# Instance norm over 512 volumes: rows of 48 KiB in four slots in place of 32 KiB in six, and the odd eight instances moved to the start

## The chip, the cores and the metric

One core of one Trainium2 chip runs the whole program; the other cores are idle. The time is the device time of one execution in microseconds. A time below is the median of some runs of one kernel unless it says otherwise, and the span is what the profiler sees from the first to the last instruction, some 1.7 us less than the time. A run is slow when it is over 1.5% above the fastest run of its kernel, and fast otherwise; only fast runs are compared.

In the profiles DVE is VectorE, ACT is ScalarE, PE is TensorE, and SP is the sync engine, which issues the loads here. A slot is a buffer for one tile. The 16 DMA engines move the data; a hole is a stretch in which one of them has nothing to move.

## The reference

```python
def reference(x, eps):            # x: (8, 64, 32, 64, 64) float32, eps = 1e-5
    mean = np.mean(x, axis=(2, 3, 4), keepdims=True)
    var = np.var(x, axis=(2, 3, 4), keepdims=True)
    return ((x - mean) / np.sqrt(var + eps)).astype(np.float32)
```

There are 512 instances of 131072 elements. Input and output are 268.4 MB each, so 536.9 MB must move at the least, every element once in and once out.

## The kernel before

A tile is 8 instances, 16 partitions each, 8192 elements (32 KiB) a partition. Six slots of that size are filled, normalized in place and stored. SP issues loads as soon as the store of the same slot has landed; ACT issues stores.

```python
    COLS = 8192
    SLOTS = 6
    FULL = P * COLS // n_elem                # 8 instances in a tile
    # ... cut
    def on_vector(eng, t, lane, n, c1, c2, c16):
        w = t.shape[1] // 2
        a = small[lane]
        eng.reduce_sum(out=a[:, 0:1], in_=t[:, :w], ...)        # half of the sum
        # after the matmul with the averaging matrix: minus the mean
        eng.tensor_reduce(out=a[:, 2:3], in_=psum[lane][:, 0:2], op=Alu.add, negate=True, ...)
        # after ACT's root: 1/root, shift = -mean/root, then half of the scaling
        eng.reciprocal(...); eng.tensor_mul(...)
        eng.tensor_scalar(out=t[:, w:], in0=t[:, w:], scalar1=a[:, 5:6], scalar2=a[:, 6:7], ...)

    def on_scalar(eng, t, lane, n, c1, c2, c16, dst):
        # ... other half of the sum; all squares (x - mean)^2; root; other half of the scaling
        eng.dma_start(out=dst, in_=t)._wait_ge(done[lane], c2).then_inc(stored[lane], 16)
    # ... cut: the last tile is done as two halves of 4 instances, 16 KiB rows
    def load_all(eng):
        for s in range(SLOTS):
            eng.dma_start(out=slots[s][:], in_=x_t[s]).then_inc(landed[s], 16)
        with eng.Fori(1, ROUNDS) as it:
            for s in range(SLOTS):
                eng.dma_start(out=slots[s][:], in_=x_t[it * SLOTS + s])._wait_ge(
                    stored[s], c16
                ).then_inc(landed[s], 16)
        # ... cut
```

Of the kernel before, what the change touches and what calls it, by code (L numbers as in the profile page):

```python
# [9 lines left out]
def kernel(  # L10
# [6 lines left out]
    nc = tc.nc  # L17
    fp32 = mybir.dt.float32
    Alu = mybir.AluOpType
    Act = mybir.ActivationFunctionType  # L20

    P = 128
    B, C, D, H, W = x.shape
    n_inst = B * C
    n_elem = D * H * W
    eps_f = float(eps)

    COLS = 8192
    SLOTS = 6
    FULL = P * COLS // n_elem  # L30
    n_tiles = n_inst // FULL
    ROUNDS = (n_tiles - 1) // SLOTS
    LANES = SLOTS + 2

    x_f = x.rearrange("b c d h w -> (b c) (d h w)")
    out_f = out.rearrange("b c d h w -> (b c) (d h w)")
    x_t = x_f.rearrange("(k i) (s f) -> k (i s) f", i=FULL, s=P // FULL)
    out_t = out_f.rearrange("(k i) (s f) -> k (i s) f", i=FULL, s=P // FULL)
    x_h = x_f.rearrange("(k i) (s f) -> k (i s) f", i=FULL // 2, s=2 * P // FULL)
    out_h = out_f.rearrange("(k i) (s f) -> k (i s) f", i=FULL // 2, s=2 * P // FULL)  # L40

    ctx.enter_context(tc.tile_critical(name="norm"))  # L42

    def sbuf(name, shape, dtype=fp32):
        return ctx.enter_context(nc.sbuf_tensor(name, shape, dtype))

    slots = [sbuf(f"slot{s}", [P, COLS]) for s in range(SLOTS)]

    unused = sbuf("unused", [P, COLS], mybir.dt.uint8)
    eps_t = sbuf("eps_t", [P, 1])  # L50
    avg = {n: sbuf(f"avg{n}", [P, P]) for n in (FULL, FULL // 2)}
    small = [sbuf(f"small{i}", [P, 8]) for i in range(LANES)]
    psum = [
        ctx.enter_context(nc.psum_tensor(f"psum{i}", [P, 512], fp32))
        for i in range(LANES)
    ]

    def semaphores(name, n):
        return [ctx.enter_context(nc.semaphore(f"{name}{i}")) for i in range(n)]

    ready = semaphores("ready", 1)[0]
    landed = semaphores("landed", LANES)
    summed = semaphores("summed", LANES)
    meaned = semaphores("meaned", LANES)
    centred = semaphores("centred", LANES)
    squared = semaphores("squared", LANES)
    varied = semaphores("varied", LANES)
    rooted = semaphores("rooted", LANES)
    scaled = semaphores("scaled", LANES)
    shifted = semaphores("shifted", LANES)  # L70
    done = semaphores("done", LANES)
    stored = semaphores("stored", LANES)



    def on_vector(eng, t, lane, n, c1, c2, c16):
        w = t.shape[1] // 2
        a = small[lane]
        eng.reduce_sum(  # L79
            out=a[:, 0:1], in_=t[:, :w], axis=mybir.AxisListType.X  # L80
        )._wait_ge(landed[lane], c16).then_inc(summed[lane], 1)
        eng.tensor_reduce(  # L82
            out=a[:, 2:3],
            in_=psum[lane][:, 0:2],
            axis=mybir.AxisListType.X,
            op=Alu.add,
            negate=True,
        )._wait_ge(meaned[lane], c1).then_inc(centred[lane], 1)
        eng.reciprocal(out=a[:, 5:6], in_=a[:, 4:5])._wait_ge(  # L89
            rooted[lane], c1  # L90
        ).then_inc(scaled[lane], 1)
        eng.tensor_mul(out=a[:, 6:7], in0=a[:, 2:3], in1=a[:, 5:6])._wait_ge(  # L92
            scaled[lane], c1
        ).then_inc(shifted[lane], 1)
        eng.tensor_scalar(  # L95
            out=t[:, w:],
            in0=t[:, w:],
            scalar1=a[:, 5:6],
            scalar2=a[:, 6:7],
            op0=Alu.mult,  # L100
            op1=Alu.add,
        )._wait_ge(shifted[lane], c1).then_inc(done[lane], 1)

    def on_scalar(eng, t, lane, n, c1, c2, c16, dst):
        w = t.shape[1] // 2
        a = small[lane]
        eng.activation(  # L107
            out=unused[:, w : 2 * w],
            in_=t[:, w:],
            func=Act.Identity,  # L110
            accum_out=a[:, 1:2],
        )._wait_ge(landed[lane], c16).then_inc(summed[lane], 1)
        eng.activation(  # L113
            out=unused[:, : 2 * w],
            in_=t,
            func=Act.Square,
            bias=a[:, 2:3],
            accum_out=a[:, 3:4],
        )._wait_ge(centred[lane], c1).then_inc(squared[lane], 1)
        eng.activation(  # L120
            out=a[:, 4:5], in_=psum[lane][:, 2:3], func=Act.Sqrt, bias=eps_t[:, 0:1]
        )._wait_ge(varied[lane], c1).then_inc(rooted[lane], 1)
        eng.activation(  # L123
            out=t[:, :w],
            in_=t[:, :w],
            func=Act.Identity,
            scale=a[:, 5:6],
            bias=a[:, 6:7],
        )._wait_ge(shifted[lane], c1).then_inc(done[lane], 1)
        eng.dma_start(out=dst, in_=t)._wait_ge(done[lane], c2).then_inc(  # L130
            stored[lane], 16
        )

    def on_tensor(eng, t, lane, n, c1, c2, c16):
        a = small[lane]
        eng.matmul(  # L136
            out=psum[lane][:, 0:2],
            lhsT=avg[n][:],
            rhs=a[:, 0:2],
            start=True,  # L140
            stop=True,
        )._wait_ge(summed[lane], c2).then_inc(meaned[lane], 1)
        eng.matmul(  # L143
            out=psum[lane][:, 2:3],
            lhsT=avg[n][:],
            rhs=a[:, 3:4],
            start=True,
            stop=True,
        )._wait_ge(squared[lane], c1).then_inc(varied[lane], 1)


    rest = [
        (x_t[k], out_t[k], slots[k % SLOTS][:], k % SLOTS, k // SLOTS + 1, FULL)
        for k in range(ROUNDS * SLOTS, n_tiles - 1)
    ]
    last = (n_tiles - 1) % SLOTS
    for h in range(2):
        k = 2 * (n_tiles - 1) + h
        half = slots[last][:, h * COLS // 2 : (h + 1) * COLS // 2]
        rest.append((x_h[k], out_h[k], half, SLOTS + h, 1, FULL // 2))  # L160

    def over_tiles(eng, step, with_target=False):
        counts = [
            ctx.enter_context(eng.register(f"{step.__name__}_c{m}")) for m in (1, 2, 16)
        ]
        for c, m in zip(counts, (1, 2, 16)):
            eng.reg_mov(c, m)
        with eng.Fori(0, ROUNDS) as it:
            for s in range(SLOTS):
                more = (out_t[it * SLOTS + s],) if with_target else ()  # L170
                step(eng, slots[s][:], s, FULL, *counts, *more)
            for c, m in zip(counts, (1, 2, 16)):
                eng.reg_add(c, c, m)
        for _, dst, t, lane, c, n in rest:
            more = (dst,) if with_target else ()
            step(eng, t, lane, n, c, 2 * c, 16 * c, *more)

    def load_all(eng):
        for s in range(SLOTS):
            eng.dma_start(out=slots[s][:], in_=x_t[s]).then_inc(landed[s], 16)  # L180
        c16 = ctx.enter_context(eng.register("load_c16"))
        eng.reg_mov(c16, 16)
        with eng.Fori(1, ROUNDS) as it:
            for s in range(SLOTS):
                eng.dma_start(out=slots[s][:], in_=x_t[it * SLOTS + s])._wait_ge(
                    stored[s], c16
                ).then_inc(landed[s], 16)
            eng.reg_add(c16, c16, 16)
        for src, _, t, lane, c, n in rest:
            behind = lane if lane < SLOTS else last  # L190
            uses = c - 1 if lane < SLOTS else ROUNDS
            eng.dma_start(out=t, in_=src)._wait_ge(stored[behind], 16 * uses).then_inc(
                landed[lane], 16
            )

    def set_up(eng):
        count = 0
        for n, m in avg.items():
            split = P // n

            eng.memset(m[:], 1.0 / n_elem).then_inc(ready, 1)  # L201
            count += 1
            for sign in (-1, 1):
                eng.affine_select(  # L204
                    out=m[:],
                    in_=m[:],
                    pattern=[[sign * split, n], [0, split]],
                    compare_op=Alu.is_ge,
                    fill=0.0,
                    base=0 if sign < 0 else split - 1,  # L210
                    channel_multiplier=-sign,
                )._wait_ge(ready, count).then_inc(ready, 1)
                count += 1
        eng.memset(eps_t[:], eps_f).then_inc(ready, 1)  # L214
        return count + 1

    load_all(nc.sync)
    set_by = set_up(nc.gpsimd)
    over_tiles(nc.vector, on_vector)
    nc.tensor.wait_ge(ready, set_by)  # L220
    over_tiles(nc.tensor, on_tensor)
    nc.scalar.wait_ge(ready, set_by)
    over_tiles(nc.scalar, on_scalar, with_target=True)

    for s in range(SLOTS):
        uses = ROUNDS + sum(1 for r in rest if r[3] == s)
        nc.scalar.wait_ge(stored[s], 16 * uses)
    for s in range(SLOTS, LANES):
        nc.scalar.wait_ge(stored[s], 16)


# [33 lines left out]
```

## Time and profile before

| | before |
|---|---|
| time, median of 3 runs | 1248.15 us (1247.99 to 1248.22) |
| span of the profiled run | 1246.2 us |
| ACT, DVE busy | 79%, 38% |
| DMAs, rows of 32 KiB and of 16 KiB | 63 and 2 each way |
| GB/s over the span | 431 |
| last store issued | 12.5 us before the end |

The page divides the span into 40 slices; a digit is the busy share in tenths, and the DMA line gives the mean of the 16 DMA engines. The prediction below shows these lines. How to read them: when the DMA line is 9 throughout and the bytes are the fewest possible, work on the compute engines that stays hidden behind the transfers should not change the middle of the run. What is left is the cost of a packet beside its bytes, and the two ends.

### The profile page before, as it was taken

The numbers are of one execution on the slowest core, as the hardware profiler recorded it, in microseconds if no ns is written. First come the engines' busy times: TensorE is split into PE (matmuls) and PEld (weight loads), VectorE is DVE, ScalarE is ACT, GpSimd is POOL, SyncE is SP. The second block draws the span as 40 slices with busy tenths as digits, with TensorE's granted clock in tenths as the row PEclk, the third lists the DMA queues.
The fourth block names the chain that finished last, engine by engine and source line by source line (L and its number), as shares of the span: only waits on it lengthen the run. The fifth ranks groups of instructions, "written<-read, shape, count | busy, mean of one in ns | idle before, by whom it ended". The sixth has DMA issues, their size and how long they took to land.

```text
span 1246.2 us, 1808 instructions
## 1 busy us (share of the span) xinstructions
PE 76.4 (6%) x260; PEld 65.2 (5%) x260; DVE 468.0 (38%) x325; ACT 986.1 (79%) x410; POOL 1.9 (0%) x11
## 2 busy tenths in 40 slices
PE   0000000000000000000000000000000000000000
PEld 0000000000000000000000000000000000000000
DVE  2344334433334334343343433434334333343331
ACT  5888888887787878778777877787787778878774
POOL 0000000000000000000000000000000000000000
DMA  9999999999999999999999999999999999999998
GB/s 404 421 438 428 430 438 436 428 431 438 435 429 431 438 435 429 431 436 436 429 431 436 436 429 430 438 436 426 433 438 436 426 433 438 435 425 435 438 429 380
DMA packets 18722, 536.90 MB, mean 431 GB/s; under 512 B 2080, under 2 KB 2080, under 8 KB 2080
## 3 DMA queue, kind: packets, MB, share of 16 engines
q1 hardware_dynamic: 9360, 268.44, 50.0%
q10 hardware_dynamic: 9360, 268.44, 49.9%
q14 instruction: 2, 0.02, 0.0%
HBM read 268.44 MB, written 268.44 MB: 431 GB/s over the span
## 4 chain that ended last, share of the span: by engine, by line
ACT 48%; DVE 29%; another core or an unknown queue 13%; PE 6%; issue 1%; DMA 1%; ACTq 0%; DVEq 0%; SPq 0%
ACT unused L113 37%; DVE small L79 18%; DVE slot L95 8%; ACT slot L123 4%; ACT unused L107 4%; PE psum L136 3%; PE psum L143 3%; ACT small L120 1%; ACT L120 1%; DMA slot<-in_x_dram 1%; DVE small L89 1%; DVE small L82 1%; DVE small L92 1%; ACTq L130 0%
## 5 line engine op out<-in xcount | busy, mean ns | idle before, releaser
L113 ACT ACTIVATE unused<-slot,small 128x8192 uint8<-128x8192 f32 (+1 forms) x65 | 456.1, 7016 | 90.2 <-DVE small L82 90.2
L79 DVE TENSOR_REDUCE small<-slot 128x1 f32<-128x4096 f32 (+1 forms) x65 | 283.0, 4353 | 163.7 <-DMA slot<-in_x_dram 163.7
L107 ACT ACTIVATE unused<-slot 128x4096 uint8<-128x4096 f32 (+1 forms) x65 | 231.7, 3564 | 81.9 <-DMA slot<-in_x_dram 76.7
L123 ACT ACTIVATE slot<-slot,small 128x4096 f32<-128x4096 f32 (+1 forms) x65 | 243.7, 3749 | 27.6 <-DVE small L92 27.6
L89 DVE RECIPROCAL small<-small 128x1 f32<-128x1 f32 x65 | 10.6, 164 | 533.8 <-ACT small L120 533.8
L95 DVE TENSOR_SCALAR slot<-slot,small 128x4096 f32<-128x4096 f32 (+1 forms) x65 | 154.7, 2380 | 2.4
L136 PE MATMUL psum<-small,avg 128*128 128x2 f32 x130 | 38.2, 363 | 673.9 <-DVE small L79 548.5
L136 PEld LDWEIGHTS psum<-small,avg 128*128 128x128 f32 x130 | 32.6, 311 | 679.4 <-DVE small L79 552.7
L143 PE MATMUL psum<-small,avg 128*128 128x1 f32 x130 | 38.2, 363 | 480.6 <-ACT unused L113 480.6
L143 PEld LDWEIGHTS psum<-small,avg 128*128 128x128 f32 x130 | 32.7, 312 | 486.1 <-ACT unused L113 486.1
L120 ACT ACTIVATE small<-psum,eps_t 128x1 f32<-128x1 f32 x65 | 17.0, 261 | 37.4 <-PE psum L143 37.3
L82 DVE TENSOR_REDUCE small<-psum 128x1 f32<-128x2 f32 x65 | 10.4, 160 | 62.8 <-PE psum L136 62.8
L107 ACT ACT_TABLE_LOAD x10 | 12.8, 1283 | 10.4 <-ACT slot L123 7.1
L120 ACT ACT_TABLE_LOAD x10 | 12.8, 1283 | 0.2
L107 ACT ACTIVATION_READ_ACCUMULATOR unused<-slot 128x1 f32 x65 | 12.1, 186 | 0.0
L113 ACT ACTIVATION_READ_ACCUMULATOR unused<-slot,small 128x1 f32 x65 | 12.1, 186 | 0.0
L92 DVE TENSOR_TENSOR small<-small 128x1 f32<-128x1 f32 x65 | 10.4, 159 | 2.2
L204 POOL TENSOR_SCALAR_AFFINE_SELECT avg<-avg 128x128 f32<-128x128 f32 x4 | 1.3, 324 | 0.3
L201 POOL MEMSET avg<- 128x128 f32 x2 | 0.4, 204 | 0.5 <-SPq L42 0.5
L246 POOL MEMSET const-bfloat16-1.0<- 128x1 bf16 x1 | 0.1, 101 | 0.0
L246 POOL MEMSET const-uint8-127<- 128x1 uint8 x1 | 0.1, 101 | 0.0
L214 POOL MEMSET eps_t<- 128x1 f32 x1 | 0.1, 99 | 0.0
(2 smaller groups left out, 0.2 us busy)
## 6 DMA issues: line engine op xcount, KB each, us to landing
slot<-in_x_dram SPq DMA_DIRECT2D x63, 4096.0 KB, 53.3
out_dram<-slot ACTq DMA_DIRECT2D x63, 4096.0 KB, 45.3
slot<-in_x_dram SPq DMA_DIRECT2D x2, 2048.0 KB, 55.6
out_dram<-slot ACTq DMA_DIRECT2D x2, 2048.0 KB, 14.7
```

The lines of the kernel that those rows point to most:

```text
L79: eng.reduce_sum(out=a[:, 0:1], in_=t[:, :w], axis=mybir.AxisListType.X)._wait_ge(landed[lane], c16).then_inc(summed[lane], 1)
L82: eng.tensor_reduce(out=a[:, 2:3], in_=psum[lane][:, 0:2], axis=mybir.AxisListType.X, op=Alu.add, negate=True,)._wait_ge(meaned[lane], c1) ...
L89: eng.reciprocal(out=a[:, 5:6], in_=a[:, 4:5])._wait_ge(rooted[lane], c1).then_inc(scaled[lane], 1)
L92: eng.tensor_mul(out=a[:, 6:7], in0=a[:, 2:3], in1=a[:, 5:6])._wait_ge(scaled[lane], c1).then_inc(shifted[lane], 1)
L95: eng.tensor_scalar(out=t[:, w:], in0=t[:, w:], scalar1=a[:, 5:6], scalar2=a[:, 6:7], op0=Alu.mult, op1=Alu.add,)._wait_ge(shifted[lane], ...
L107: eng.activation(out=unused[:, w : 2 * w], in_=t[:, w:], func=Act.Identity, accum_out=a[:, 1:2],)._wait_ge(landed[lane], c16).then_inc(sum ...
L113: eng.activation(out=unused[:, : 2 * w], in_=t, func=Act.Square, bias=a[:, 2:3], accum_out=a[:, 3:4],)._wait_ge(centred[lane], c1).then_in ...
L120: eng.activation(out=a[:, 4:5], in_=psum[lane][:, 2:3], func=Act.Sqrt, bias=eps_t[:, 0:1])._wait_ge(varied[lane], c1).then_inc(rooted[lane ...
L123: eng.activation(out=t[:, :w], in_=t[:, :w], func=Act.Identity, scale=a[:, 5:6], bias=a[:, 6:7],)._wait_ge(shifted[lane], c1).then_inc(don ...
L136: eng.matmul(out=psum[lane][:, 0:2], lhsT=avg[n][:], rhs=a[:, 0:2], start=True, stop=True,)._wait_ge(summed[lane], c2).then_inc(meaned[lan ...
L143: eng.matmul(out=psum[lane][:, 2:3], lhsT=avg[n][:], rhs=a[:, 3:4], start=True, stop=True,)._wait_ge(squared[lane], c1).then_inc(varied[la ...
L204: eng.affine_select(out=m[:], in_=m[:], pattern=[[sign * split, n], [0, split]], compare_op=Alu.is_ge, fill=0.0, base=0 if sign < 0 else s ...
```

## The change

The intent is fewer and larger DMAs. A row of 48 KiB (12288 elements) in four slots takes the same 192 KiB a partition as 32 KiB in six. But 12288 does not divide an instance of 131072, so a row holds three chunks of 4096 that may belong to two instances. Sums are therefore made per chunk, spread over three columns by a mask, averaged by the matmul, and picked up again by the mask. A tile holds 128 x 12288 elements, 12 instances; 512 instances are 42 tiles and eight instances over. These come first, in two parts of four instances with 16 KiB rows. To balance the engines, one of the three chunks of squares goes from ACT to DVE, and 1536 elements of one sum as well. An early load of ACT's table takes the place of one pair of table loads per pass of the loop.

```diff
-    COLS = 8192
-    SLOTS = 6
+    CHUNK = 4096
+    THIRDS = 3
+    COLS = THIRDS * CHUNK
+    SLOTS = 4
     ... cut
+        eng.tensor_tensor(out=block(a, by_both, n, m), in0=spread(a, at, m),
+                          in1=belongs[:, :, :m], op=Alu.mult)       # sums by instance
+        # the matmul averages, then:
+        eng.tensor_reduce(out=a[:, by_instance : by_instance + n], in_=p..., op=Alu.add)
+        eng.tensor_tensor(out=block(a, by_chunk, n, n), ..., op=Alu.mult)
+        eng.tensor_reduce(out=a[:, to : to + n], in_=block(a, by_chunk, n, n), negate=negate)
     ... cut: DVE's part of the squares
+        eng.tensor_scalar(out=chunk[0], in0=chunk[0], scalar1=column(a, MEANS, 0), op0=Alu.add)
+        eng.tensor_tensor_reduce(out=unused[2][:], in0=chunk[0], in1=chunk[0],
+                                 accum_out=column(a, SQUARES, 0), ...)
     ... cut: loads
+        for m, (lane, t) in enumerate(parts):                       # two parts first
+            eng.dma_start(out=t, in_=part_of(x_f, m)).then_inc(landed[lane], 16)
         for s in range(SLOTS):
-            eng.dma_start(out=slots[s][:], in_=x_t[s]).then_inc(landed[s], 16)
+            load = eng.dma_start(out=slots[s][:], in_=x_t[s])
+            if s >= SLOTS - n_parts:
+                load._wait_ge(stored[s + n_parts], 16)
+            load.then_inc(landed[s], 16)
     ... cut
+    nc.scalar.preload_act_table(Act.Sqrt)
```

## The prediction

> **What bounds the kernel now.** I read the page first, then the waits of the compute engines and of the loading queue, then the end of the timeline, then the packet records of the trace. The page's strip over 40 slices comes first:
>
> ```profile
> ACT  5888888887787878778777877787787778878774
> DMA  9999999999999999999999999999999999999998
> GB/s 404 421 438 428 430 438 436 428 431 438 435 429 431 438 435 429 431 436 436 429 431 436 436 429 430 438 436 426 433 438 436 426 433 438 435 425 435 438 429 380
> DMA packets 18722, 536.90 MB, mean 431 GB/s; under 512 B 2080, under 2 KB 2080, under 8 KB 2080
> ...
> q1 hardware_dynamic: 9360, 268.44, 50.0%
> q10 hardware_dynamic: 9360, 268.44, 49.9%
> ```
>
> The DMA row is 9 in every slice but the last, and the two queues' packets fill 99.9% of the 16 engines' span. The bytes are the least possible: every element is read once and written once. ACT, the busiest engine, has idle tenths everywhere. The packet count tells what a packet is: 9360 = 65 DMAs x (128 rows + 16 semaphore writes), so a partition's row is one packet (32 KiB; 16 KiB in the halves).
>
> The chain of waits looks different, and must not be misread:
>
> ```profile
> ACT 48%; DVE 29%; another core or an unknown queue 13%; PE 6%; issue 1%; DMA 1%; ACTq 0%; DVEq 0%; SPq 0%
> ```
>
> It walks through a tile's latency (sums, squares, scale), because a load waits for a store and a store for its tile. Latency bounds nothing while the DMA engines have other queued work. The waits say that they have:
>
> ```profile
> DVE small L79 <- DMA slot<-in_x_dram: 163.7, 53, 13.2
> ...
> ACT unused L107 <- DMA slot<-in_x_dram: 76.7, 44, 8.6
> ```
>
> ```profile
> SPq L185 <- DMA out_dram<-slot: 1048.9, 54, 50.6
> ```
>
> The compute engines wait for loads, loads wait for slots, slots wait for stores. Late in the run a tile takes as long as its transfers:
>
> ```profile
> 1174.73 3.62 ACT L107 ACTIVATE unused<-slot 128x4096 uint8<-128x4096 f32 x1 [1.73 <-DMA slot<-in_x_dram]
> ...
> 1192.43 0.35 ACTq L130 DMA_DIRECT2D out_dram<-slot  x1
> 1194.11 3.62 ACT L107 ACTIVATE unused<-slot 128x4096 uint8<-128x4096 f32 x1 [1.70 <-DMA slot<-in_x_dram]
> ...
> 1233.70 0.34 ACTq L130 DMA_DIRECT2D out_dram<-slot  x1
> ```
>
> Tiles start 19.4 us apart; from data to store takes 17.7 us. 8.39 MB in 19.4 us is 432 GB/s. The last store is issued 12.5 us before the end, though its 2 MB need only 4.9 us: earlier stores still fill the engines. So even the tail has no DMA hole. This kernel is at the DMA's rate from about 2 us to the end; only the cost per packet and the two ends can change.
>
> **What the Trainium skill says.** "DMA: Bandwidth & Descriptors", section Where 436 GB/s comes from: 16 ports x 32 B x 850 MHz = 435.2 GB/s. The trace agrees: 433 GB/s between 100 and 1200 us, 99.5% of it. Same page, Why small descriptors are slow: a fixed overhead of about 3 cycles per packet[...]. The trace shows one of that order. Landings of consecutive loads beside stores are 19.362 us apart, which is 16 packets of 32 KiB, so 1.2101 us each; the last two stores, alone, land 4.863 us apart, which is 8 packets of 16 KiB, 0.6079 us each. The line through both is 0.6022 us per 16 KiB plus 5.7 ns per packet. Same page, Queues, rings and completion order: an engine takes turns between queues, a packet at a time. The trace agrees: the first of the two half loads, 16 KiB rows against 32 KiB rows of a store, landed 14.54 us after its predecessor, and 8 x (0.608 + 1.210) = 14.54. "VectorE: DVE Perf Modes", section Mode 2x_2P: an fp32 operation of a tensor with scalars makes two results a cycle, one of two tensors only one. Here a tensor-with-scalar pass of 4096 takes 2.41 us and a sum of 4096 takes 4.42; no row of before shows two large tensors.
>
> **The change part by part.**
>
> (1) Packets. 42 tiles of 48 KiB rows and two parts of 16 KiB rows: per engine 42 x 16 = 672 large packets and 32 small, in place of 1008 of 32 KiB and 32 of 16 KiB. If a 48 KiB row stays one packet it takes 3 x 0.6022 + 0.0057 = 1.812 us (estimate, from that line). Before: 1008 x 1.2101 + 32 x 0.6079 = 1239.2 us. After: 672 x 1.8123 + 32 x 0.6079 = 1237.3 us. Gain 1.9 us. This is the only part that acts on the bound.
>
> (2) Compute per tile, now against 16 x 1.812 = 29.0 us of transfers. ACT: sums 3.62 + 2.34 (2560 elements, from 3.62 for 4096 and 1.91 for 2048), squares 2 x 3.71, four accumulator reads of 0.19, root 0.3, scale 3.80, issue 0.4: 18.6 us. DVE: sums 4.42 + 1.76 (1536, same way), eight small mask steps and two others of about 0.2, centring 2.41, product with itself 4.6 (guess: the sum's rate plus an accumulator read), two scalings of 2.41: 20.0 us. Both under 29.0, at 64% and 69%; ACT goes down from 79%, DVE up from 38%. The 20 table loads (25.6 us) vanish but one. All beside the DMA; worth nothing.
>
> (3) Latency of a tile: sums 6.4; mask, matmul and three small steps 1.5 (a matmul round is 0.7); squares 7.8 on ACT (7.1 on DVE); again 1.5; root, reciprocal, product 0.8; two scalings on DVE 4.9: 22.9 us, in place of 17.7.
>
> (4) Start. Data begin at 2.05 us as before. The parts land at about 7 and 12 us. The first is ready 10.2 us (as the halves in before) after its data are seen, so the first store is issued near 19, against 31.6. Loads queue all that time, so this fills no hole, it only fixes how far stores run behind loads.
>
> (5) Tail, which decides the sign. From the start, by turns of a packet: stores enter at about 24 us; a 16 KiB store packet against a 48 KiB load packet is 2.42 us a pair, so the parts' stores end near 43 and 63; tile 0 has landed at 27, tile 1 at 46, tile 2 at 67. Then pairs of 3.62 us, 29.0 per tile: load k ends at 67 + 29(k - 2), store k at 92 + 29k. Load k+4 is issued near 93.5 + 29k and needed at 96 + 29k, so the load queue just stays fed. Load 41 ends at 1198; store 39 then has 6.8 of its 8 packets to go and store 40 all 8: 14.8 x 1.81 = 26.8 us of work alone. The last tile needs about 2.4 us until all engines' landings are seen, 22.9 us of compute and 1.0 to its first packet: 26.3 us. So the hole is about nought, with no margin. Before had halves there.
>
> Sum: 1246.2 - 1.9 + hole. I put the hole at 1 us (the recurrence says 0, errors can only open it): span 1245.3, and the measured time is 1.95 above the span in before (1248.15 against 1246.2): 1247.2 us.
>
> **The rivals.** (a) A tail hole. Had stores run closer behind loads, each us of that phase would open half a us; without the 28 us by which stores queue in my recurrence it would be 14 us: 1260 us. Against: the slots hold loads back, so stores stay behind. (b) A 48 KiB row is cut into packets. In three of 16 KiB: 672 x 2 more at 5.7 ns, +7.7 us, 1255. For it: no packet above 32 KiB was seen. Against: nothing shows a limit, 16 and 32 KiB rows were not cut. (c) The product with itself takes two passes on DVE: +4.4 us of DVE, 24.4 of 29.0, still hidden, but latency +3.7, so the same in the tail: 1251. (d) Four slots are too few: the load queue runs dry every round. A slot's cycle of 116 us must hold 29 + 29 of transfers, 23 of compute and some 4 of latencies; 31 are over. DMA has the other queue to serve meanwhile. Nought. (e) Larger packets lift the rate more than the line says. Against: 0.5% to the ceiling is all there is, about 6 us: 1242.
>
> **Range and chances.** The ceiling alone, 536.9 MB at 435.2 GB/s, is 1233.6 us; with the ends of before (7 us: 2.05 at the start, 5.0 at the end and in the store's start) the span can hardly be under 1240.6, 1242.6 as a time. That is 0.4% below before: faster by 2% is shut out. 2% slower is 1273, which needs (a) at its worst together with (b). Range 1243.5 to 1252, longer above than below because the hole opens one way only. Faster 0.01, same 0.97, slower 0.02.
>
> **What would show it.** (1) right: 5632 + 704 packets, half of them a queue, tiles 29.0 us apart; wrong: over 17,000 packets. (2) ACT near 64% and DVE near 69%. (3) 22.9 us between a tile's first sum and its store. (4) first store issued at 19 us. (5) GB/s of the last slices as high as before; a hole shows as a last slice well under 380 and the last store issued over 15 us before the end with nothing left ahead of it. I am wrong if the steady rate leaves 433 to 434 GB/s, or the hole is over 5 us.

## The result, and the profile after

| | before | after |
|---|---|---|
| time, median of 6 runs each on the same chip | 1248.12 us (1247.99 to 1250.38) | 1246.83 us (1246.76 to 1249.90) |
| span of the profiled run | 1246.2 us | 1245.2 us |
| ACT, DVE busy | 79%, 38% | 61%, 65% |
| DMA packets | 18722 | 12674 |
| data to store, one whole tile | 17.7 us | 21.9 us |

A ratio is the mean time of one kernel's fast runs over that of the other's in the same rounds, so it is not quite the ratio of the medians in the table. Here it is 0.9991 with a 95% interval from 0.9978 to 1.0004: the same within 2%, and not clear of one. Five runs of six on each side lie within 0.25 us of each other, and these two groups are 1.3 us apart; the sixth was 2 to 3 us longer.

The page of the changed kernel, its strip and its packets:

```profile
DVE  2887666666666666666666666666666666666663
ACT  5876555566666665665556665666566555566653
...
DMA  9999999999999999999999999999999999999998
GB/s 396 429 430 434 444 433 429 431 429 441 439 433 431 429 429 444 436 429 433 431 433 442 434 431 431 429 434 444 433 431 431 429 442 437 431 433 429 429 444 368
DMA packets 12674, 536.89 MB, mean 431 GB/s; under 512 B 1408, under 2 KB 1408, under 8 KB 1408
...
q1 hardware_dynamic: 6336, 268.44, 49.9%
q10 hardware_dynamic: 6336, 268.44, 49.8%
```

There are 44 DMAs each way x (128 rows + 16 semaphore writes) = 6336 packets a queue: a row of 48 KiB stayed one packet. DMA is 9 in the same slices as before. In the last slice it moved 368 GB/s against 380.

Who waited for whom, compute engines first, the loading queue second:

```profile
ACT unused L213 <- DMA slot<-in_x_dram: 308.1, 40, 8.2
DVE small L157 <- DMA slot<-in_x_dram: 279.6, 40, 7.4
```

```profile
SPq L357 <- DMA out_dram<-slot: 1024.6, 36, 29.2
```

The loop is the same one: compute waits for loads, loads wait for stores. The compute engines now wait for data in 40 of 42 whole tiles. ACT waits 308 us in place of 77: the time saved on ACT has become waiting. DVE waits 280 us in place of 164 although it does more.

The end of the timeline (start, length, engine, line, operation, count, and the idle time before it):

```profile
1176.70 3.62 ACT L213 ACTIVATE unused<-slot 128x4096 uint8<-128x4096 f32 x1 [7.96 <-DMA slot<-in_x_dram]
...
1198.60 0.35 ACTq L240 DMA_DIRECT2D out_dram<-slot  x1
1205.76 3.62 ACT L213 ACTIVATE unused<-slot 128x4096 uint8<-128x4096 f32 x1 [7.94 <-DMA slot<-in_x_dram]
1205.76 6.08 DVE L157 TENSOR_REDUCE small<-slot 128x1 f32<-128x4096 f32 x2 [7.19 <-DMA slot<-in_x_dram]
...
1215.74 4.42 DVE L171 CUSTOM_DVE_ANT_0 unused<-slot 128x4096 uint8<-128x4096 f32 x1
...
1227.65 0.35 ACTq L240 DMA_DIRECT2D out_dram<-slot  x1
```

Tiles start 29.06 us apart, data to store takes 21.9 us, and the last store is issued 17.5 us before the end, where a 6 MB store alone needs 8 x 1.812 = 14.5. The square of the DVE chunk (the custom operation) takes 4.42 us, as long as a sum of the same size.

The trace also holds each packet, and for each DMA the completion of each of its 16 engines. These records are the finest tool, so here is what they give, in a table of their own. A packet's record is 3 ns longer than the step to the next one, so 1815 ns in the records is 1812 in a sum. The records do not name the engine; where single engines are told apart below, packets were joined into 16 chains, each to the one that had just ended. "First" and "last" are the earliest and the latest of the 16 engines to complete the last whole or half load; their difference is called the lag.

| | before | after |
|---|---|---|
| median packet: 16, 32, 48 KiB | 611, 1213, - ns | 611, -, 1815 ns |
| loads apart, first engine | 19.362 us per 32 KiB tile | 29.000 us per 48 KiB tile |
| last load complete, first / last engine | 1220.84 / 1222.76 us | 1202.88 / 1205.26 us |
| lag there | 1.9 us | 2.4 us |
| last store complete, first / last engine | 1242.67 / 1244.67 us | 1243.07 / 1243.43 us |

The steady step is 1.5 x 19.362 = 29.043 us before for the same bytes as 29.000 after. Over 42.7 such steps that is 1.8 us.

In the tail of the changed kernel the first engine completes the last store but one at 1226.45 us and the last engine at 1228.93. The next store takes 14.5 us. On that first engine it begins at 1228.66 and completes at 1243.20, so this engine had a hole of 2.2 us; on the last it completes at 1243.43, so there the hole is nought. Engine by engine, 14 had a hole of 0.9 to 2.2 us, and the two that were furthest behind had none; one of these ended the run. In the kernel before no engine had a hole there.

### The profile page after: what moved, and what is told of

It is laid out like the page before. It is cut to its first block, busy times and chain, and to the rows that moved or that the text cites. A ratio compares the mean times of both kernels' runs of the same rounds, so it can differ in the third digit from the quotient of the medians.

```text
span 1245.2 us, 1950 instructions
## 1 busy us (share of the span) xinstructions
PE 52.7 (4%) x176; PEld 44.1 (4%) x176; DVE 811.6 (65%) x724; ACT 757.7 (61%) x433; POOL 2.7 (0%) x15
## 2 busy tenths in 40 slices
DMA packets 12674, 536.89 MB, mean 431 GB/s; under 512 B 1408, under 2 KB 1408, under 8 KB 1408
## 3 DMA queue, kind: packets, MB, share of 16 engines
q1 hardware_dynamic: 6336, 268.44, 49.9%
q10 hardware_dynamic: 6336, 268.44, 49.8%
## 4 chain that ended last, share of the span: by engine, by line
another core or an unknown queue 82%; DMA 9%; DVE 3%; ACT 2%; SPq 1%; issue 1%; PE 0%; ACTq 0%
DMA slot<-in_x_dram 6%; DMA out_dram<-slot 4%; ACT unused L220 2%; SPq L357 1%; DVE small L157 1%; DVE slot L200 1%; DVE slot L193 1%; ACT unused L213 0%; PE psum L250 0%; DVE small L137 0%; DVE small L125 0%; DVE small L131 0%; DVE small L143 0%; SPq L355 0%
## 5 line engine op out<-in xcount | busy, mean ns | idle before, releaser
L213 ACT ACTIVATE unused<-slot 128x4096 uint8<-128x4096 f32 x84 | 249.3, 2968 | 310.5 <-DMA slot<-in_x_dram 308.1
L157 DVE TENSOR_REDUCE small<-slot 128x1 f32<-128x4096 f32 x84 | 255.3, 3081 | 279.6 <-DMA slot<-in_x_dram 279.6
L220 ACT ACTIVATE unused<-slot,small 128x4096 uint8<-128x4096 f32 x84 | 310.8, 3701 | 65.3 <-DVE small L143 65.3
L171 DVE CUSTOM_DVE_ANT_0 unused<-slot 128x4096 uint8<-128x4096 f32 x42 | 185.9, 4426 | 1.4
L233 ACT ACTIVATE slot<-slot,small 128x4096 f32<-128x4096 f32 x42 | 159.7, 3802 | 18.5 <-DVE small L188 18.5
L200 DVE TENSOR_SCALAR slot<-slot,small 128x4096 f32<-128x4096 f32 x42 | 101.1, 2408 | 0.0
L164 DVE TENSOR_SCALAR slot<-slot,small 128x4096 f32<-128x4096 f32 x42 | 98.8, 2353 | 1.5
L250 PE MATMUL psum<-small,avg 128*128 128x12 f32 (+1 forms) x168 | 50.4, 375 | 1144.3 <-DVE small L125 1144.3
L193 DVE TENSOR_SCALAR slot<-slot,small 128x4096 f32<-128x4096 f32 x42 | 98.6, 2347 | 0.0
L250 PEld LDWEIGHTS psum<-small,avg 128*128 128x128 f32 x168 | 42.1, 311 | 1152.5 <-DVE small L125 1152.5
L125 DVE TENSOR_TENSOR small<-small,belongs 128x12 f32<-128x12 f32 x84 | 14.3, 170 | 31.9 <-ACT unused L220 29.5
L137 DVE TENSOR_TENSOR small<-small,belongs 128x9 f32<-128x9 f32 x84 | 14.3, 170 | 2.9
L289 ACT ACTIVATE unused<-slot,small 128x4096 uint8<-128x4096 f32 x2 | 7.4, 3707 | 2.0 <-DVE small L266 2.0
```

Source lines behind the costliest of these rows:

```text
L125: eng.tensor_tensor(out=block(a, by_both, n, m), in0=spread(a, at, m), in1=belongs[:, :, :m], op=Alu.mult,)._wait_ge(*wait).then_inc(steps ...
L137: eng.tensor_tensor(out=block(a, by_chunk, n, n), in0=spread(a, by_instance, n), in1=belongs[:, :, :n].rearrange("p i c -> p c i"), op=Alu ...
L157: eng.reduce_sum(out=column(a, SUMS, j), in_=part, axis=AXIS)._wait_ge(landed[lane], c16).then_inc(summed[lane], 1)
L164: eng.tensor_scalar(out=chunk[0], in0=chunk[0], scalar1=column(a, MEANS, 0), scalar2=None, op0=Alu.add,)._wait_ge(centred[lane], c1).then_ ...
L171: eng.tensor_tensor_reduce(out=unused[2][:], in0=chunk[0], in1=chunk[0], scale=1.0, scalar=0.0, op0=Alu.mult, op1=Alu.add, accum_out=colum ...
L193: eng.tensor_scalar(out=chunk[0], in0=chunk[0], scalar1=column(a, SCALES, 0), scalar2=None, op0=Alu.mult,)._wait_ge(scaled[lane], c1).then ...
```

## The experiments

All were compared with the kernel before on the same chip in the same call, where its medians lay between 1248.07 and 1248.17 us. The changed kernel was not in these calls, so a comparison with its 1246.8 us is one across calls. Medians are often some us above the lowest run here, so both are given.

**Smaller packets, all else kept.** Every tile's load and store become three DMAs of 16 KiB rows.

```diff
-        eng.dma_start(out=dst, in_=t)._wait_ge(done[lane], c3).then_inc(stored[lane], 16)
+        for i in range(THIRDS):
+            cut = slice(i * CHUNK, (i + 1) * CHUNK)
+            store = eng.dma_start(out=dst[:, cut], in_=t[:, cut])
+            if i == 0:
+                store._wait_ge(done[lane], c3)
+            store.then_inc(stored[lane], 16)
```

> The changed kernel, but each tile's load and store are three DMAs of 16 KiB rows, waited for together. Theory 1 (the gain is the cost per packet, 5.7 ns each, on a bound of DMA time): 2048 packets of 0.6079 us an engine make 1245.0 us in place of 1237.3, so tiles 29.18 us apart in place of 29.00 and a time of about 1254.5 us. Theory 2 (the gain of 1.3 us comes from the ends, the two parts first instead of two halves last): no change, 1246.8 us.

Measured: 1257.67 us, lowest 1255.56. The page:

```profile
DMA packets 36866, 536.90 MB, mean 427 GB/s; under 512 B 4096, under 2 KB 4096, under 8 KB 4096
```

Loads of a third are 9.724 us apart on the first engine, so 29.17 us a tile against an expected 29.18 and against 29.00: 7.3 us over the run, where the cost per packet says 7.7. The run is 3.2 us longer than expected. In the trace 1.3 us are a larger lag (3.7 us in place of 2.4 at the last load), and 1.9 are a hole that even the last engine has: the last engine completes the earlier stores at 1237.48 us, and the last tile's store is issued at 1238.53 and starts at 1239.4. 7.3 + 1.3 + 1.9 = 10.5; the spans differ by 10.7. Theory 2, no change, falls; that packets cost what the line says is shown in the rate, while what the ends give between the two kernels is not measured here.

**The order alone, in the kernel before.** The two halves come first instead of last.

```diff
-    for h in range(2):                       # two halves after the whole tiles
-        k = 2 * (n_tiles - 1) + h
-        ...
-        rest.append((x_h[k], out_h[k], half, SLOTS + h, 1, FULL // 2))
+    first = [(x_h[h], out_h[h], slots[SLOTS - 2 + h][:, : COLS // 2], SLOTS + h, 1, FULL // 2)
+             for h in range(2)]              # done and loaded before the loop
```

> The kernel before (32 KiB rows, six slots) with its two halves moved from the end to the start, nothing else. Theory 1 (packets): DMA time stays 1239.2 us and no hole opens in the tail (latency 21 us against 21 us of queued stores), so 1248.1 us, at most 1 off. Theory 2 (ends): the order takes the gain, 1246.8 us.

Measured: 1248.13 us in the profiled run, but 1254.06 to 1257.92 in the five others (median of all six 1255.27).

> The same kernel as in the run with the halves first, for a profile of one of its slower runs (1254 to 1258 us; the first profile fell on the one of 1248.1). Theory (one DMA engine falls behind the other 15 by slow packets): in a slow run the first engine's landings stay 19.36 us apart, the last engine's lag grows to some 9 us at the end instead of 2, and mean packet time is above its median. Rival (a hole in the tail, from the order of the tiles): the lag stays near 2 us and the last store starts late.

Measured: 1247.96 in the profiled run, 1253.93 to 1256.45 in the four others. So no slow run was profiled. The two profiled runs agree with theory 1 (1248.1 expected; lag 2.1 us at the last load of the first of them), and no run of eleven came near the 1246.8 of theory 2, so the order alone does not bring the gain at 32 KiB rows. One part of theory 1 was wrong: 15 engines of the first profile have a hole of 0.9 to 1.9 us before the last store. The one that ends the run has none. The nine other runs are 6 to 10 us longer than either theory says, on two chips; why is open, the two profiled runs cannot stand for them, and the expectation about the lag is untested.

**The order alone, in the changed kernel.** The two parts come last.

```diff
-        for m, (lane, t) in enumerate(parts):
-            eng.dma_start(out=t, in_=part_of(x_f, m)).then_inc(landed[lane], 16)
         ... the whole tiles, then
+        for m, (lane, t) in enumerate(parts):
+            behind = SLOTS - n_parts + m
+            eng.dma_start(out=t, in_=part_of(x_f, m))._wait_ge(
+                stored[behind], 16 * len(range(behind, n_tiles, SLOTS))
+            ).then_inc(landed[lane], 16)
```

> The changed kernel with its two parts at the end instead of the start. Theory 1 (packets): the same packets; the last part needs 10.4 us of compute while some 15 us of stores are queued, so no hole: 1246.8 us, at most 1 off. Theory 2 (ends): the gain is lost, 1248.1 us or more.

Measured: 1249.17 us, lowest 1247.62; the profiled run took 1252.29. The lowest agrees with theory 1 within its margin, the median does not. In the profiled run the lag was 5.4 us at the last whole tile, and packets of 48 KiB took 1819.6 ns in the mean, 4.6 above their median of 1815, which is 3.1 us over 672 of them. The verdict between the theories is inconclusive, since the median came out where theory 2 put it; but in the trace the engine that ends the run, at 1248.94 us, has no hole in the tail. Fourteen others have holes of 1.8 to 3.5 us and are done by 1245.1. So lag and slow packets end this run, not a hole that the order made.

**Longer tiles.** One needless sum of 4.4 us in every whole tile.

```diff
+        eng.reduce_sum(out=column(a, 70, 0), in_=chunk[1], axis=AXIS)
         eng.tensor_scalar(out=chunk[1], in0=chunk[1], scalar1=column(a, SCALES, 1), ...)
```

> The changed kernel with one needless DVE sum of 4096 (4.4 us) between the two scalings of every whole tile. Theory 1 (DMA bound; latency counts once, in the tail): tiles stay 29.0 us apart, the last store is issued 4.4 us later, at about 1232, and begins at 1233 where the slowest engine had run out of stores at 1228.9: a hole of 4, time 1251.0 us. Rival (the chain of waits is the bound): 4.4 us in each of 10 to 11 rounds of slots, about 1293 us.

Measured: 1253.69 us; two of the five runs took 1251.05 and 1251.07. The timeline's last issues, of the profiled run (1253.79):

```profile
1176.69 0.34 ACTq L241 DMA_DIRECT2D out_dram<-slot  x1
1205.80 0.35 ACTq L241 DMA_DIRECT2D out_dram<-slot  x1
...
1234.87 0.35 ACTq L241 DMA_DIRECT2D out_dram<-slot  x1
```

Stores stay 29.1 us apart with 4.4 us more work in each tile, and on the first engine loads are 29.000 us apart: the chain of waits does not bound the body (the rival's 1293 us are 40 away). The last store is issued 7.2 us later than in the changed kernel. 4.4 is the pass, and 2.9 a larger lag of the last engine at the last load (5.25 us against 2.38), which together make 7.3. The span grew by 6.9. So in this run latency of the last tile and lag of the last engine both come out in the end almost one for one. On the last engine itself the hole is 3.9 us (its store but one completes at 1231.81, the last begins at 1235.7), against an expected 4. The two lowest runs are at the expected 1251.0.

**Longer tiles, parts last.** Both edits together.

> The needless 4.4 us of DVE in every whole tile, with the two parts at the end instead of the start. Theory (the 4.4 us cost only where the last tile's latency outlasts the queued stores): the last things are now parts of 10 us latency, so the 4 us come back: as the kernel with parts last and no extra pass, 1247.6 us in its fastest run, against 1251.05 with parts first. Rival (the extra pass costs by load on DVE or bandwidth): 4 us stay, 1251 or more in the fastest run.

Measured: 1259.86 us, lowest 1257.38. That is 9.8 us above the theory's figure, and 6.3 above the 1251 of the rival, whose "or more" it meets. The page's queues and the last issue in the timeline:

```profile
q1 hardware_dynamic: 6336, 268.44, 49.9%
q10 hardware_dynamic: 6336, 268.44, 49.4%
```

```profile
1246.72 0.34 ACTq L307 DMA_DIRECT2D out_dram<-slot  x1
```

The two queues' packets fill 99.3% of the engines' span, but with slower packets: 1827 ns in the mean for 48 KiB, 12 above the median, 8.1 us over 672 packets. Lag jumps to 6.2 us at the fourth load, and is 16.4 us at the last part. The extra pass keeps DVE no busier than in the experiment with longer tiles (79% in both), and that one had no such slow packets (mean 1817 ns). So neither theory explains it, and the run does not test what it was made for. In one profile each, both kernels with the parts last have slower packets (1820 and 1827 ns in the mean, against 1816 to 1817 in four profiles with the parts first) and a larger greatest lag of a load (6.1 and 16.4 us, against 2.4 to 5.3); why is open.

**Only load and store.** Three kernels without arithmetic, with the tile sizes 32 KiB x 6, 48 KiB x 4 and 64 KiB x 3. Their outputs are wrong, which doesn't matter for the times. Only the one with 48 KiB rows has the two parts: 32 and 64 KiB divide the data into 64 and 32 whole tiles, unlike what the first expectation says.

```diff
-    over_tiles(nc.vector, ...); over_tiles(nc.tensor, ...); over_tiles(nc.scalar, ...)
+    for k in range(n_tiles):
+        s, c = k % SLOTS, k // SLOTS
+        load = nc.sync.dma_start(out=slots[s][:], in_=x_t[k])     # waits for stored[s]
+        ...
+        nc.scalar.dma_start(out=out_t[k], in_=slots[s][:])._wait_ge(
+            landed[s], 16 * (c + 1)
+        ).then_inc(stored[s], 16)
```

> On purpose no normalization (a wrong result): load and store alone, 32 KiB rows in six slots, a store waits only for its own load; two parts of 16 KiB rows first. Theory (DMA time is all): the same packets as the kernel before, 1239.2 us an engine, no hole; so a time of about 1248, as with the arithmetic. Rival (the arithmetic costs bandwidth, by sharing the memory of the slots or by its waits): clearly under 1246.

Measured: 1247.26 us (1246.98 to 1247.61).

> Load and store alone, a wrong result on purpose: 48 KiB rows in four slots, two parts first, the packets of the changed kernel: 1237.3 us an engine. Theory: about 1246.8 us, or 1246 as the 2 us hole of most engines in the tail goes; 1 to 2 us under the copy with 32 KiB rows. Rival (the gain has to do with the arithmetic or the tail, not with packets): equal to the copy with 32 KiB rows.

Measured: 1246.68 us over six fast runs (1244.98 to 1250.79), and one slow, 1438.86 us, on which the profile fell.

> The same copy with 48 KiB rows, for a profile of a fast run (the first fell on one of 1438.9 us). Theory: a fast run (1245 to 1248) has tiles 29.00 us apart on all engines, a lag of at most 3 us, and packets at their median of 1815 ns; the slow one had a mean of 1906 ns and a lag of 34 us. Rival: the lag is there in fast runs too and does not matter.

Measured: 1249.25 us (1245.09 to 1259.84, four runs); the profile fell on one of 1247.65.

> Load and store alone, a wrong result on purpose: 64 KiB rows in three slots. Theory: if such a row stays one packet, 512 packets of 4 x 0.6022 + 0.0057 = 2.4145 us make 1236.2 us, 1.1 under the copy with 48 KiB rows, so about 1245.5; the gain shrinks with each step. If rows are cut at some size below 64 KiB, the packet count says so and the gain is gone.

Measured: 1257.43 us (1248.17 to 1261.19, six runs); the profile fell on one of 1260.59.

The line of GB/s of each page, in the order 32, 48 (slow), 48 (fast), 64 KiB; of the last the packet count too:

```profile
GB/s 387 437 430 429 438 436 427 434 438 434 425 438 437 433 427 438 437 428 431 438 436 423 438 437 434 426 438 437 429 430 438 436 425 436 438 434 425 438 437 388
```

```profile
GB/s 393 430 434 435 434 431 425 427 361 372 372 372 365 368 367 373 373 367 372 358 380 383 364 358 352 352 372 372 364 379 372 372 368 369 365 378 365 393 265 189
```

```profile
GB/s 397 428 429 437 443 429 429 431 429 450 431 429 429 431 443 437 429 429 431 431 450 431 429 431 431 443 437 429 431 431 434 445 431 429 431 431 447 434 429 360
```

```profile
GB/s 400 433 431 433 431 429 435 433 429 431 431 433 433 433 435 431 435 435 429 427 439 433 427 423 433 429 433 433 433 429 435 408 431 431 431 431 433 433 408 296
DMA packets 9216, 536.88 MB, mean 426 GB/s; under 512 B 1024, under 2 KB 1024, under 8 KB 1024
```

| | median packet | mean packet | lag, fourth load | lag, last load | time of this run |
|---|---|---|---|---|---|
| 32 KiB x 6 | 1213 ns | 1214.6 ns | 1.4 us | 1.4 us | 1247.26 us |
| 48 KiB x 4, fast | 1815 ns | 1815.5 ns | 2.9 us | 5.1 us | 1247.65 us |
| 48 KiB x 4, slow | 1815 ns | 1905.8 ns | 3.6 us | 34.2 us | 1438.86 us |
| 64 KiB x 3 | 2418 ns | 2436.6 ns | 3.9 us | 27.5 us | 1260.59 us |

Three things follow. First, the arithmetic costs next to nothing: the copy with 32 KiB rows takes 0.9 us less than the kernel before, the fast copies with 48 KiB rows lie on both sides of the changed kernel. Second, the line of the prediction holds: 611, 1213, 1815 and 2418 ns are 602 to 603 ns apart, and 64 KiB is still one packet (32 tiles x 144 packets x 2 = 9216). Third, the lowest run falls from 1246.98 to 1244.98 from 32 to 48 KiB, about the 1.9 us of the packets, but the runs spread by 0.6, then 14.9 (1244.98 to 1259.84, fast ones only), then 13.0 us. The medians, 1247.26 against 1246.68 and 1249.25, do not decide between theory and rival, and at 64 KiB the expected 1245.5 us was missed: the lowest run is 2.7 above it. In the slow run of 48 KiB one engine or more fell a whole tile behind, and single packets take up to 2.4 us on top of 1.8; as no fast run shows that, nothing is built on it. The expectation of a lag of at most 3 us in a fast run was wrong: it was 5.1, 4.7 of it there by the eleventh load. Row size and number of slots change together in this series, so which of them makes the spread is not told apart.

**The last store in three pieces.** Each chunk of the last tile is stored as soon as it is scaled.

```diff
+        if last:
+            eng.dma_start(out=dst[:, 2 * CHUNK :], in_=chunk[2])._wait_ge(cut[2], 1).then_inc(stored[lane], 16)
+            return
     ... and on SP, for the two other chunks
+        for j in range(2):
+            at = slice(j * CHUNK, (j + 1) * CHUNK)
+            eng.dma_start(out=out_t[n_tiles - 1][:, at], in_=slots[end][:, at])._wait_ge(cut[j], 1)...
```

> The changed kernel, but the last tile is stored in three DMAs of 16 KiB rows, each as soon as its chunk is scaled (two issued by SP, one by ACT), which starts its first store about 2.4 us earlier. Theory (the one lagging DMA engine sets the end and has no hole in the tail): nothing gained, 1246.8 us, at most 0.4 less. Rival (the 2.1 us hole that 15 engines have in the tail sets the end): 2 us gained, 1244.8 us.

Measured: 1247.09 us (four runs from 1246.90 to 1247.20, one of 1249.52). The last issues of the profiled run:

```profile
1225.54 3.02 SPq L374 DMA_DIRECT2D out_dram<-slot  x2
1227.12 0.35 ACTq L242 DMA_DIRECT2D out_dram<-slot  x1
```

The first of the three is issued at 1225.54 us, 2.1 before the 1227.65 of the changed kernel, and the time is no shorter (1247.09 against 1246.83). So the hole of most engines (14, not the 15 that the expectation has) costs nothing here; the engine that lags sets the end.

**The changed kernel once more**, on chip 10. The record does not name the chip of the first comparison, and this run was made on the same day, unlike what the expectation says.

> The changed kernel itself once more, on another day's chip share, to settle whether its 1.3 us are real. Theory: most runs within 0.2 of 1246.8 us against 1248.1 of before, with a rare run 2 to 3 us longer on either side. Rival (noise): medians overlap.

Measured: 1248.39 us (1246.82, 1247.16, 1248.39, 1249.73, 1250.30) against 1248.07 (nine runs from 1247.99 to 1248.28); ratio 1.0003, interval 0.9989 to 1.0017. The rival is nearer: the medians do not keep their order. The profile fell on the run of 1248.39. There the first engine completes the last load at 1202.88 us as in the first profile, to a hundredth; the last engine at 1206.88, a lag of 4.0 in place of 2.4 us. That is 1.6 us, and the time is 1.5 longer than in the first profile.

## Why the prediction was right

The time was predicted as 1247.2 us, with a range from 1243.5 to 1252; it was 1246.83 first, and 1248.39 later. What carried it is that the DMA engines bound the kernel and that only the cost per packet and the ends can move it. By steps:

- (1) Packets: right. 48 KiB stayed one packet; 29.000 us a tile against 28.997 expected; 1.8 us of gain against 1.9. The experiment with rows in three (29.17 us a tile, 29.18 expected) and the copies confirm the line from 16 to 64 KiB. The count named as a sign, 5632 + 704 packets, is that of one queue and not, as the text has it, of both.
- (2) Compute: right that it is worth nothing. ACT came to 61% (64 expected), DVE to 65% (69 expected).
- (3) Latency: 21.9 us against 22.9 expected. Each term was put a little too high: the sums took 6.1 us and not 6.4, the squares 7.5 and not 7.8, the scalings 4.7 and not 4.9.
- (4) Start: the first store was issued at 19.3 us, 19 expected.
- (5) Tail: near in size, wrong in its working. Load 41 was expected to end at 1198 us and ended at 1202.9 on the first engine, since load 2 had got 5 packets and not 6.8 by the time the parts' stores were over (it ended at 71.9 us in place of 67). Then 13 packets of stores were queued in place of 14.8, 3.2 us less; against this the latency was 1.0 shorter. So 14 engines had a hole of up to 2.2 us where "about nought, with no margin" stood. On the one engine that sets the end the hole was nought after all, for it was 2.4 us behind and still had stores.
- The sum, "span 1245.3", met 1245.2. But its terms are not the ones that the trace has: the packets' -1.8, no hole on the engine that counts, and about 0.8 more at the ends and from that engine's lag (2.4 in place of 1.9 us at the last load). The hole of 1 us stood for these, so that the sum met to 0.1 us is luck. Also, 1.95 us from span to time is the median of three runs less the span of a fourth; that fourth run took 1247.95 us, so it should have been 1.7, and the sum gives 1247.0.
- The rivals: (b), (c) and (d) did not come true (for (c), the product with itself took 4.42 us, one pass); (a) was shown in kind by the experiment with longer tiles, where 4.4 us of latency cost 4.3 in the lowest runs (1251.05 against 1246.76); (e) is out, since the packets lie on the line.

What the prediction did not have at all is that the lag differs from one run of a kernel to another: 2.4 us at the last load in one profile of the changed kernel, 4.0 in the other, and 1.5 us more time. It carried "the ends of before" over as a constant 5.0 us. For the kernel before that is fair (40 of its 44 runs, the first six and the 38 made beside the experiments, lie between 1247.92 and 1248.44 us); for the changed kernel 3 of 11 runs lie above 1249.5. So of the packets' 1.8 us some 1.3 reach the time in the good runs. In the other profiled run lag used them up; that it did so in the unprofiled long runs is likely and not shown. What makes an engine lag, and whether larger rows or fewer slots make it worse, stays open.

## What to carry to other kernels

When the DMA line is full from end to end and the bytes are minimal, work out the packet count before restructuring the arithmetic: here a third fewer packets was worth 1.8 us of 1248 by the rate, and no gain was found from anything else in a large rewrite. In these runs the last tile's latency counted once, and only by as much as it outlasted the stores still queued on the slowest DMA engine. Look at the completion of all 16 engines and at more than one run: a change of a tenth of a per cent can be smaller than how far one engine falls behind.

## What the Trainium skill lacked or had wrong

- "DMA: Bandwidth & Descriptors", section Why small descriptors are slow: it has a fixed overhead of about 3 cycles per packet, worked out for a descriptor of 256 bytes. At the 850 MHz that the page gives for the fabric this would be 3.5 ns, an estimate. The runs show 5.7 ns a packet, of which 0.7 is its share of the semaphore writes (6 ns from start to start, one for eight rows), for rows of 16 to 64 KiB, where it is still worth 1.8 us of 1248.
- The same page, section SWDGE vs HWDGE vs iDMA: its table of what GpSimd builds has a packet as "≤4096 B preferably", and the section gives no size for DMAs issued from SP and ACT. The runs of such DMAs show a row as one packet at 16, 32, 48 and 64 KiB: 611, 1213, 1815 and 2418 ns.
- No page that I read says how far one of the 16 DMA engines falls behind the others when both directions are full, or that this differs between runs of one kernel. In the profiled fast runs here it is 1.4 to 6.1 us at most for a load in most, 16 and 28 us in two, and the two profiles of the changed kernel, with 2.4 and 4.0 us at the last load, took 1246.88 and 1248.39 us.
